# Decays and scaled operands of the recurrent heads made in the projection stage; closing sums of attention on GpSimd and ScalarE

## The chip, the cores and the metric

The kernel runs on one core of a Trainium2 chip as one program. The metric is the device time of one execution in microseconds. Inputs and outputs are float32 in DRAM.

## The reference, cut to what matters

One encoder layer runs over two sequences, 2048 and 256 tokens, of width 1024. A joint projection feeds two mixers side by side: differential attention (4 heads) and a bidirectional RWKV-7 recurrence (8 heads of 64, both directions). The mixed output is projected back, and a squared-ReLU feed-forward of width 4096 follows, each with a residual.

```python
z = rms_norm(x, norm1_g) @ w_in                    # 3328 columns: 1536 attention, 1792 recurrent
# attention: q, k normed and rotated; two softmaxes per head
attn = softmax(q0 k0) - lam * softmax(q1 k1); o = rms_norm(attn @ v, subln_g) * (1 - lambda_init)
# recurrence, d = direction, w_dn/a_dn/g_dn low-rank parts of z after mixing with neighbours
w_log = -softplus(-(w0[d] + tanh(w_dn) @ w_up[d])) - 0.5
decay = exp(-exp(w_log))
a_rate = sigmoid(a0[d] + a_dn @ a_up[d])
kk = normalised(k * k_k);  k_dir = k * (1 + (a_rate - 1) * k_a)
state = state * decay + (state @ -kk) outer (kk * a_rate) + v outer k_dir;  y = state @ r
x = x + concat(o, gate(normed(y) + bonus)) @ w_out
x = x + relu(rms_norm(x, norm2_g) @ w_ff1) ** 2 @ w_ff2
```

## The kernel before, in words

18 tiles of 128 tokens (16 of the long sequence, 2 of the short) go through four stages. Matrix products of the big weights are split into a high and a low part and done in three passes. A scheduler at build time lays out the order of each engine's queue: it takes instructions in program order where it can and moves others up when their inputs and buffers are free by its own estimate of times. Every transfer is issued by SyncE, whose queue is in order as well.

**Projection.** `project_stream` takes two groups of nine tiles. `tall` makes recurrent columns transposed, 128 columns by 384 tokens at a time; `wide` makes attention columns, two tiles by 256 columns per PSUM bank, three banks in turn (tag `mm`). For q and k the result goes to `rope` (L308 on): a Square on ScalarE (L324), a sum on VectorE (L326), a power on GpSimd (L90), the normed tile `qn` (L330, the last reader of the bank), products with cosine and sine (`t1` L333, `t2` L336), their sum (L340), a split into two parts, transposes, a store. `sq` and `t2` share the tag `rsq`. The column blocks of attention go in the order 512, 1024, 768, 1280, 0, 256; blocks under 1024 have a rope for every two tiles, five per block; the last two run as a pair with ten ropes in a row. Weights of a step are loaded in four pieces through `w_raw`, one step ahead.

Between the yields of this stream, `rw_prep` runs for nine blocks of two tiles. It mixes each recurrent column with its neighbours in time (`mix`: one ScalarE and two VectorE operations), makes the low-rank rates for four groups of 128 columns (loop over `c`), and stores plain operands to DRAM: r (RR), kk (KK), k and b of both directions (KB), tanh of the decay's low rank (TW), v (V).

**Attention beside the recurrence.** `merge` in program order interleaves 72 attention items (head, tile) with 18 recurrent units. An item's scores go through VectorE (maximum), ScalarE (exponential), GpSimd and VectorE (difference of the two softmaxes), TensorE (transpose and product with v), and `attn_out` closes it (L640 on). A recurrent unit treats a tile in each direction: `rw_inter` (L873 on) loads the stored operands, makes the decay (a matmul `lp`, tanh, a scan in chunks of 64, two exponentials), multiplies r, kk, k and b by it into `ar` and `bk`, and makes masked scores (`scp`, L935) and transposes; `rw_leaf` inverts 32x32 triangles, `rw_merge` joins them, `rw_chain` runs the state. Preparation is two units ahead of the chain.

**Output projection** (`wout`) and **feed-forward** (`mlp`) follow.

## Time and profile before

| what | us |
|---|---|
| median of 3 runs (4057.95 to 4066.89) | 4065.56 |
| profiled execution, its own time | 4069.43 |
| its span, first to last instruction | 4067.6 |
| TensorE busy / VectorE busy | 3841.0 / 2535.4 |
| ScalarE busy / GpSimd busy | 1904.9 / 1249.5 |
| mean granted clock of TensorE | 0.969 |

Busy time of TensorE is modelled and overlaps from one matmul to the next, so a busy TensorE need not be at its peak. The granted clock is a share of 2.4 GHz. "Idle before" of a group is the time in which its engine stood still just ahead of it, and the arrow names what ended that.

### The profile page before, as it was taken

What the parts mean: (1) busy time and instruction counts of PE and PEld (TensorE: products, weight loads), DVE (VectorE), ACT (ScalarE), POOL (GpSimd) and SP (SyncE); (2) the same over time, 40 slices, a digit from 0 to 9 for tenths busy, and PEclk for the clock granted to TensorE, in tenths of its full rate; (3) what the DMA queues carried; (4) which work ended last, traced back from release to release, by engine and by line L of the source; (5) the groups of instructions that cost most, each with busy time, mean ns of one, the idle gap of its engine ahead of it and who ended that gap; (6) DMA issues with size and microseconds to landing.
All of it is one profiled execution on the core that took longest, in us unless ns stands there. A gap on an engine that the chain in (4) does not pass through costs nothing.

```text
span 4067.6 us, 75970 instructions
## 1 busy us (share of the span) xinstructions
PE 3841.0 (94%) x28790; PEld 3428.7 (84%) x28790; DVE 2535.4 (62%) x5080; ACT 1904.9 (47%) x4312; POOL 1249.5 (31%) x1632
## 2 busy tenths in 40 slices
PE   8999998988889888889897999999999999999999
PEld 8999998976777677777776778999999999999998
DVE  4254767679878878788885775444444444444443
ACT  4354555467666656566665224333333333333332
POOL 0023666556656556556554440000000000000000
PEclk9999998999989989889998999999999999999999
DMA  6366666643443343334324376222252222521221
GB/s 188 121 198 194 199 178 195 181 108 73 111 95 83 94 119 90 85 85 112 89 62 151 105 234 200 63 68 67 63 186 63 64 66 65 158 63 63 63 63 39
DMA packets 617558, 458.05 MB, mean 113 GB/s; under 512 B 232498, under 2 KB 569191, under 8 KB 617192
## 3 DMA queue, kind: packets, MB, share of 16 engines
q1 hardware_dynamic: 617192, 453.20, 38.9%
q8 instruction: 227, 3.72, 0.4%
q14 instruction: 139, 1.14, 0.1%
HBM read 323.98 MB, written 129.07 MB: 111 GB/s over the span
## 4 chain that ended last, share of the span: by engine, by line
PE 54%; DVE 11%; POOL 6%; DMA 4%; issue 3%; ACT 2%; SPq 1%; POOLq 0%; DVEq 0%; ACTq 0%
PE ups L102 7%; PE ups L100 7%; PE ups L101 7%; PE yps L102 6%; PE yps L101 6%; PE yps L100 6%; DVE nb L591 2%; PE oo L637 2%; PE wops L101 2%; PE wops L100 2%; PE wops L102 2%; POOL lx L964 1%; DMA XD<-lx 1%; POOL ltmp L962 1%; DVE lx L964 1%
## 5 line engine op out<-in xcount | busy, mean ns | idle before, releaser
L504 DVE TENSOR_TENSOR acc<-yps,acc 128x512 f32<-128x512 f32 x576 | 392.0, 688 | 374.8 <-PE yps L102 374.8
L100 PE MATMUL ups<-h2hi,f_hi 128*128 128x384 f32 x1536 | 515.6, 336 | 0.0
L102 PE MATMUL ups<-h2hi,f_lo 128*128 128x384 f32 x1536 | 515.6, 336 | 0.0
L101 PE MATMUL ups<-h2lo,f_hi 128*128 128x384 f32 x1536 | 515.3, 335 | 0.0
L595 ACT ACTIVATE P<-sc,nb 128x512 f32<-128x512 f32 (+1 forms) x528 | 360.2, 685 | 218.4 <-DVE nb L591 203.2
L101 PE MATMUL yps<-f_lo,uh 128*128 128x512 f32 x1152 | 449.8, 391 | 0.0
L100 PE MATMUL yps<-f_hi,uh 128*128 128x512 f32 x1152 | 449.6, 391 | 0.0
L102 PE MATMUL yps<-f_hi,ul 128*128 128x512 f32 x1152 | 442.8, 391 | 0.0
L137 ACT CAST f_hi<-f_raw 128x1024 fp32r<-128x1024 f32 x96 | 96.2, 1048 | 646.7 <-PE yps L102 645.3
L591 DVE TENSOR_REDUCE nb<-sc 128x1 f32<-128x512 f32 (+1 forms) x528 | 345.2, 671 | 56.7 <-PE sc L589 55.6
L637 PE MATMUL oo<-vv,at 128*128 128x128 f32 x2080 | 307.0, 294 | 31.5 <-ACT at L634 20.6
L637 PEld LDWEIGHTS oo<-vv,at 128*128 128x128 f32 x2080 | 272.1, 202 | 60.9 <-ACT at L634 31.6
L588 PE MATMUL sc<-kt,qq 128*128 128x512 f32 (+1 forms) x528 | 253.3, 480 | 49.0 <-ACT P L595 42.1
L492 DVE TENSOR_TENSOR ul<-u,uh 128x384 fp32r<-128x384 f32 x192 | 106.8, 556 | 299.8 <-ACT uh L491 296.3
L101 PEld LDWEIGHTS ups<-h2lo,f_hi 128*128 128x128 f32 x1536 | 288.2, 188 | 5.7
L102 PEld LDWEIGHTS ups<-h2hi,f_lo 128*128 128x128 f32 x1536 | 288.2, 188 | 5.5
L100 PEld LDWEIGHTS ups<-h2hi,f_hi 128*128 128x128 f32 x1536 | 288.3, 188 | 5.5
L102 PEld LDWEIGHTS yps<-f_hi,ul 128*128 128x128 f32 x1152 | 216.1, 188 | 47.4
L143 DVE SCALAR_TENSOR_TENSOR f_lo<-f_raw,g,f_hi 128x256 fp32r<-128x256 f32 x384 | 168.7, 481 | 138.6 <-ACT f_hi L142 138.5
L100 PE MATMUL mm<-w_hi,hT_hi 128*128 128x256 f32 x864 | 250.2, 290 | 4.9 <-DVE qn L330 4.2
L100 PEld LDWEIGHTS yps<-f_hi,uh 128*128 128x128 f32 x1152 | 216.3, 188 | 39.3
L101 PE MATMUL mm<-w_lo,hT_hi 128*128 128x256 f32 x864 | 249.0, 289 | 0.0
(236 smaller groups left out, 9313.0 us busy)
## 6 DMA issues: line engine op xcount, KB each, us to landing
f_raw<-w_ff SPq DMA_DIRECT2D x192, 256.0 KB
f_raw<-w_ff SPq DMA_DIRECT2D x96, 512.0 KB
w_raw<-w_in SPq DMA_DIRECT2D x104, 256.0 KB
qq<-QT SPq DMA_DIRECT2D x288, 64.0 KB
kb<-KB SPq DMA_DIRECT2D x36, 512.0 KB
ZT<-zs SPq DMA_DIRECT2D x84, 192.0 KB
xt<-x SPq DMA_DIRECT2D x27, 512.0 KB
zr<-ZT SPq DMA_DIRECT2D x18, 516.0 KB
```

What stands on the lines that cost most here:

```text
L100: mm(ps, lh, rh, start=start, stop=False)
L101: mm(ps, lh, rl, start=False, stop=False)
L102: mm(ps, ll, rh, start=False, stop=stop)
L137: nc.scalar.copy(hi[:, ks], raw)
L143: nc.vector.scalar_tensor_tensor(out=lo[:, k], in0=raw[:, k - k0], scalar=gk, in1=hi[:, k].bitcast(F32), op0=ALU.mult, op1=ALU.subtract)
L492: nc.vector.tensor_tensor(out=ul[:, ns], in0=u2, in1=uh[:, ns].bitcast(F32), op=ALU.subtract)
L504: nc.vector.tensor_tensor(out=acc[j][:, cs], in0=ps, in1=acc[j][:, cs], op=ALU.add)
L588: nc.tensor.matmul(sc, qq[:, c, 0], kt, start=True, stop=False)
L591: nc.vector.tensor_reduce(out=m, in_=sc, axis=AX.X, op=ALU.max, negate=True)
L595: nc.scalar.activation(out=P, in_=sc, func=AF.Exp, bias=m, accum_out=(a["ls"][:, hf] if a["nh"] > 1 else a["l"])[:, c:c + 1])
L637: nc.tensor.matmul(a["op"], at[:, b], a["kv"][1][hf][:, b], start=k == 0, stop=k == a["n"] - 1)
L964: e.tensor_tensor(out=X[:, 0:i, k0:16], in0=X[:, 0:i, k0:16], in1=tmp[:, 0:i, 0:n], op=ALU.add)
```

## The change

The decay and the products with it move from `rw_inter` into the loop over `c` of `rw_prep`. It makes both directions at once, 256 tokens per column group, and stores the scaled operands in the form in which the score matmuls read them: AR and BK take the place of RR, KK, KB and TW. The products of the decay's low rank use a high and a low part in place of one float32 product. V is stored per column group and tile. To make room, several tags go down to one buffer (`rsq`, `hlT`, `kb`), `w_raw` from three to two, and the r vectors are made per column group. In `rw_inter` the two heads' score products no longer alternate. The indices of a tile's two halves are swapped for the backward direction in `rw_chain`. `attn_out` uses GpSimd for the sums and ScalarE for the scaling.

```diff
-            raw = (rp or sp).tile([128, st, shape[2]], F32, name=tag + "_raw", tag=tag + "_raw", bufs=3)
+            raw = (rp or sp).tile([128, st, shape[2]], F32, name=tag + "_raw", tag=tag + "_raw", bufs=RAWB[tag])
...
-        sq = sp.tile([128, m * n, 64], F32, name="rsq", tag="rsq")
+        sq = sp.tile([128, m * n, 64], F32, name="rsq", tag="rsq", bufs=RSQ)
...
-        t2 = sp.tile([128, m, n, 64], F32, name="t2", tag="rsq")
+        t2 = sp.tile([128, m, n, 64], F32, name="t2", tag="rsq", bufs=RSQ)
...
-            hT = sp.tile([128, n, m, 128], F32R, name="hlT", tag="hlT")
+            hT = sp.tile([128, n, m, 128], F32R, name="hlT", tag="hlT", bufs=1)
...
-        nc.vector.scalar_tensor_tensor(out=rs, in0=l0, scalar=1e-6, in1=l0, op0=ALU.mult, op1=ALU.mult)
-        nc.vector.scalar_tensor_tensor(out=rs, in0=ss, scalar=1.0 / 128, in1=rs, op0=ALU.mult, op1=ALU.add)
+        nc.gpsimd.tensor_scalar(out=rs, in0=l0, scalar1=l0, scalar2=1e-6, op0=ALU.mult, op1=ALU.mult)
+        nc.gpsimd.tensor_scalar(out=rs, in0=ss, scalar1=1.0 / 128, scalar2=rs, op0=ALU.mult, op1=ALU.add)
         nc.gpsimd.tensor_tensor(out=rs, in0=rs, in1=self.halfneg[:, 0:1], op=ALU.pow)
         o = sp.tile([128, 128], F32, name="o", tag="ao", bufs=1)
-        nc.vector.tensor_scalar(out=o, in0=op, scalar1=rs, scalar2=None, op0=ALU.mult)
+        nc.scalar.activation(out=o, in_=op, func=AF.Copy, scale=rs)
...
+            for j in range(n):
+                nc.sync.dma_start(out=self.V[t0 + j * 128:t0 + j * 128 + 128].rearrange("p (h c i) -> p h c i", h=2, c=4)[:, :, c], in_=vt[:, j])
...
+                for nm, x, o, bias in (("w_up", (wh, wl), lw, self.w0h), ("a_up", (ah, al), th, self.a0h)):
+                    aps = pp.tile([128, W], F32, name="aps", tag="w512")
+                    aw = wp[nm][:, d, c * 128:c * 128 + 128]
+                    nc.tensor.matmul(aps, aw, x[0], start=True, stop=False)
+                    nc.tensor.matmul(aps, aw, x[1], start=False, stop=True)
+                    nc.scalar.activation(out=o[:, d], in_=aps, func=AF.Tanh, scale=0.5, bias=bias[:, d * 4 + c:d * 4 + c + 1])
+            nc.gpsimd.tensor_scalar(out=lw, in0=lw, scalar1=CDEC, scalar2=CDEC, op0=ALU.mult, op1=ALU.add)
...
+            for d in range(2):
+                x = lw[:, d]
+                nc.vector.tensor_tensor_scan(out=x[:, ::-1] if d else x, data0=self.chunk[:, 0:W], data1=x[:, ::-1] if d else x,
+                                             initial=0.0, op0=ALU.mult, op1=ALU.add)
+                nc.scalar.activation(out=eg[:, d, 0:nq, 1:65], in_=x.rearrange("p (q t) -> p q t", t=64), func=AF.Exp)
+                nc.scalar.activation(out=en[:, d], in_=x, func=AF.Exp, scale=-1.0)
+                e = 1 if d else 64
+                nc.gpsimd.tensor_copy(self.pcs[:, s0 + b0:s0 + b0 + n, d, c], eg[:, d, 0:nq, e:e + 1].rearrange("p (j x) o -> p j (x o)", x=2))
...
+            ar = sp.tile([128, nq, 2, 2, 64], F32, name="aro", tag="aro", bufs=1)
+            nc.gpsimd.tensor_tensor(out=ar[:, :, :, 1].rearrange("p q d t -> p d q t"), in0=rf.rearrange("p (q t) -> p q t", t=64).unsqueeze(1).to_broadcast([128, 2, nq, 64]),
+                                    in1=eg[:, :, 0:nq, 1:65], op=ALU.mult)
+            for d in range(2):
+                nc.vector.scalar_tensor_tensor(out=ar[:, :, d, 0], in0=kq[:, :, ::-1] if d else kq, scalar=-0.5,
+                                               in1=eg[:, d, 0:nq, 65:1:-1] if d else eg[:, d, 0:nq, 0:64], op0=ALU.mult, op1=ALU.mult)
...
+            nc.sync.dma_start(out=self.AR[:, qs, :, c].rearrange("p q d k -> p (q d) k"), in_=ar.rearrange("p q d o t -> p (q d) (o t)"))
+            bk = sp.tile([128, nq, 2, 2, 64], F32, name="kb", tag="kb", bufs=1)
+            for d in range(2):
+                b = bk[:, :, d, 1]
+                nc.vector.scalar_tensor_tensor(out=b[:, :, ::-1] if d else b, in0=th[:, d].rearrange("p (q t) -> p q t", t=64), scalar=1.0, in1=kq, op0=ALU.add, op1=ALU.mult)
+                e = en[:, d].rearrange("p (q t) -> p q t", t=64)
+                nc.vector.tensor_tensor(out=b, in0=b, in1=e[:, :, ::-1] if d else e, op=ALU.mult)
+            nc.gpsimd.tensor_scalar(out=th, in0=th, scalar1=self.ka2[:, cs], scalar2=self.ka1[:, cs], op0=ALU.mult, op1=ALU.add)
...
+            nc.gpsimd.tensor_tensor(out=kd, in0=th, in1=kf[:, c:c + 1].to_broadcast([128, 2, W]), op=ALU.mult)
+            nc.gpsimd.tensor_tensor(out=bk[:, :, :, 0].rearrange("p q d t -> p d q t"), in0=kd.rearrange("p d (q t) -> p d q t", t=64), in1=en.rearrange("p d (q t) -> p d q t", t=64), op=ALU.mult)
+            dst = self.BK[:, qs, :, c].rearrange("p q d k -> p (q d) k")
+            nc.sync.dma_start(out=dst[64:128], in_=bk[64:128].rearrange("p q d s t -> p (q d) (s t)"))
+            for z in range(2):
+                nc.sync.dma_start(out=dst[0:64, :, 64 - 64 * z:128 - 64 * z], in_=bk[0:64, :, :, z].rearrange("p q d t -> p (q d) t"))
...
-        nc.sync.dma_start(out=tw, in_=self.TW[:, ts])
...
-            nc.sync.dma_start(out=ar[:, :, x, 1], in_=self.RR[:, :, t * 128 + xn * 64:t * 128 + xn * 64 + 64].rearrange("c p t -> p c t"))
...
-        nc.sync.dma_start(out=kb, in_=self.KB[:, :, :, d, ts])
...
-            nc.tensor.matmul(lp[:, c], self.wup[:, d, c * 128:c * 128 + 128], tw, start=True, stop=True)
...
-        nc.vector.tensor_tensor_scan(out=en.rearrange("p a b -> p (a b)"), data0=self.chunk, data1=lw[:, ::-1] if d else lw,
...
+        ar, bk = (sp.tile([128, 2, 4, 2, 64], F32, name=nm, tag=nm, bufs=b) for nm, b in (("ar", R), ("bk", 2)))
+        for o, src in ((ar, self.AR), (bk, self.BK)):
+            nc.sync.dma_start(out=o.rearrange("p x c s t -> p x (c s t)"), in_=src[:, 2 * t:2 * t + 2, d].rearrange("p x c k -> p x (c k)"))
...
-            nc.vector.tensor_tensor(out=bk[b, :, :, s], in0=view(kb[b, :, s]), in1=en4[b], op=ALU.mult)
...
+        nc.gpsimd.tensor_copy(pc[:, d], self.pcs[:, t, d, :, ::-1] if d else self.pcs[:, t, d])
...
-            pss = [pp.tile([128, 4, 128], F32, name="scp", tag=SCPT, bufs=WB) for h in range(2)]
-            for c in range(4):
-                for h in range(2):
-                    hs = slice(h * 64, h * 64 + 64)
-                    nc.tensor.matmul(pss[h][:, c], bk[hs, c, x].rearrange("p s t -> p (s t)"),
+            for h in range(2):
+                hs = slice(h * 64, h * 64 + 64)
+                ps = pp.tile([128, 4, 128], F32, name="scp", tag=SCPT, bufs=WB)
+                for c in range(4):
+                    nc.tensor.matmul(ps[:, c], bk[hs, c, x].rearrange("p s t -> p (s t)"),
                                      ar[hs, c, x].rearrange("p s t -> p (s t)"), start=True, stop=True)
-            for h in range(2):
-                nc.vector.tensor_tensor(out=sc[:, h, 4 * x:4 * x + 4], in0=pss[h], in1=self.mask[:, d * (1 + h):d * (1 + h) + 1].to_broadcast([128, 4, 128]), op=ALU.mult)
+                nc.vector.tensor_tensor(out=sc[:, h, 4 * x:4 * x + 4], in0=ps, in1=self.mask[:, d * (1 + h):d * (1 + h) + 1].to_broadcast([128, 4, 128]), op=ALU.mult)
...
+RSQ = 1
+RAWB = {"w": 2, "f1": 3, "f2": 3}
```

## Rows read from the trace of the kernel before

**Rows 1.** Busy time by stage: stretch, us, each engine (count), clock, DMA share, GB/s
```profile
0.00:840.00 840.00, 797.59 (x5654) 784.06 (x5654) 479.57 (x1019) 401.11 (x908) 341.89 (x376) 0.98 0.60 179
840.00:2210.00 1370.00, 1198.58 (x13891) 995.67 (x13890) 1108.43 (x2502) 886.34 (x2216) 796.86 (x1169) 0.93 0.38 92
2210.00:2470.00 260.00, 251.53 (x1174) 198.09 (x1174) 189.27 (x315) 79.96 (x137) 110.24 (x88) 0.98 0.59 195
2470.00:4067.00 1597.00, 1593.31 (x8076) 1450.87 (x8073) 758.13 (x1247) 537.45 (x1054) 0.55 (x1) 1.00 0.26 82
```

**Rows 2.** Chain that ended last, shares of the whole span by engine
```profile
PE 54%; DVE 11%; POOL 6%; DMA 4%; issue 3%; ACT 2%; SPq 1%; POOLq 0%; DVEq 0%; ACTq 0%
```

**Rows 3.** Groups of instructions, VectorE, attention stage 840 to 2210 us
```profile
L900 DVE TENSOR_TENSOR_SCAN en<-chunk,lw 128x512 f32<-128x512 bf16 x36 | 49.1, 1364 | 31.5 <-POOL lw L898 31.5
L914 DVE SCALAR_TENSOR_TENSOR ar<-kk,eg 128x512 f32<-128x512 f32 x36 | 29.0, 805 | 2.5 <-ACT eg L903 2.1
L925 DVE TENSOR_TENSOR bk<-kb,en 64x512 f32<-64x512 f32 x36 | 26.8, 744 | 0.0
L927 DVE TENSOR_TENSOR bk<-kb,en 64x512 f32<-64x512 f32 x36 | 26.2, 729 | 0.5
L649 DVE TENSOR_SCALAR o<-oo,ors 128x128 f32<-128x128 f32 x72 | 24.6, 342 | 13.5 <-POOL ors L647 11.3 <-DMA MIX<-o 1.9
...
L646 DVE SCALAR_TENSOR_TENSOR ors<-oss,ors 128x1 f32<-128x1 f32 x72 | 19.2, 267 | 18.5 <-ACT osq L643 18.1
...
L645 DVE SCALAR_TENSOR_TENSOR ors<-l 128x1 f32<-128x1 f32 x72 | 17.5, 244 | 0.1
...
L917 DVE TENSOR_TENSOR ar<-ar,eg 128x512 f32<-128x512 f32 x18 | 13.6, 755 | 0.0
```

**Rows 4.** The same view, GpSimd
```profile
L922 POOL TENSOR_TENSOR bk<-kb,en 128x512 f32<-128x512 f32 x36 | 49.0, 1382 | 0.5 <-ACT en L904 0.5
L647 POOL TENSOR_TENSOR ors<-ors,halfneg 128x1 f32<-128x1 f32 x72 | 42.6, 592 | 119.3 <-DVE ors L646 116.3 <-DVE lx L964 1.7 <-DVE g L610 0.8
L917 POOL TENSOR_TENSOR ar<-ar,eg 128x512 f32<-128x512 f32 x18 | 23.2, 1291 | 12.5 <-ACT eg L903 9.3 <-DMA XD<-lx 2.9 <-DVE ltmp L962 0.3
L898 POOL TENSOR_SCALAR lw<-lw 128x512 f32<-128x512 f32 x36 | 22.3, 621 | 30.4 <-ACT lw L896 13.0 <-ACT cf L606 12.4 <-DMA MIX<-o 2.7
```

**Rows 5.** The same view, ScalarE
```profile
L903 ACT ACTIVATE eg<-en 128x512 f32<-128x512 f32 x36 | 22.7, 629 | 29.5 <-DVE en L900 26.0 <-DVE mx L604 2.5 <-DVE ors L646 0.8
```

**Rows 6.** Timeline of TensorE, attention stage: start, us, instruction, count in the run
```profile
1513.87 1.16 PE L894 MATMUL lp<-tw,wup 65*128 65x128 f32 x8
...
1530.74 1.16 PE L935 MATMUL scp<-ar,bk 64*128 64x128 f32 x16
1531.83 1.16 PE L637 MATMUL oo<-vv,at 128*128 128x128 f32 x8
...
1536.11 1.16 PE L935 MATMUL scp<-ar,bk 64*128 64x128 f32 x8
```

**Rows 7.** Busy time by stretch, second half of projection; columns as in rows 1
```profile
420.00:780.00 360.00, 338.62 (x2779) 332.43 (x2778) 261.23 (x535) 186.88 (x419) 217.46 (x225) 0.96 0.63 186
600.00:640.00 40.00, 28.94 (x185) 26.64 (x184) 37.51 (x74) 25.94 (x61) 28.51 (x34) 0.76 0.76 223
780.00:828.00 48.00, 48.00 (x416) 48.00 (x415) 23.89 (x46) 14.85 (x27) 29.78 (x23) 1.00 0.61 173
```

**Rows 8.** Groups of instructions, whole run, preparation blocks
```profile
L809 DVE SCALAR_TENSOR_TENSOR kb<-th,rsb 128x256 f32<-128x256 f32 x72 | 35.8, 509 | 21.1 <-ACT th L805 19.1 <-DMA KB<-kb 1.8
...
L805 ACT ACTIVATE th<-aps,a 128x256 f32<-128x256 f32 x72 | 33.7, 472 | 53.3 <-POOL kb L811 33.0 <-PE aps L803 17.1 <-PE mm L102 2.7
```

**Rows 9.** Timeline of all engines, one rope and the next Square
```profile
777.58 0.60 ACT L324 ACTIVATE rsq<-mm 128x512 f32<-128x512 f32 x1 [1.06 <-PE mm L102]
...
783.99 0.60 ACT L324 ACTIVATE rsq<-mm 128x512 f32<-128x512 f32 x1 [5.55 <-PE mm L102]
784.00 0.69 DVE L340 TENSOR_TENSOR t<-t,t 128x512 f32<-128x512 f32 x1 [1.87 <-POOL t L336]
```

**Rows 10.** One line of the tile w_raw: least/median/most ns, first and last start
```profile
L143 DVE SCALAR_TENSOR_TENSOR w_lo<-w_raw,g,w_hi x208: 468/480/1524, 8.7 to 776.3; 128x256 fp32r<-128x256 f32 x104
```

More of the change, by code (lines that the diff above doesn't have):

```diff
@@ L170, in rope_tables @@
             for p in range(2):
-                g = sp.tile([128, 4, 128], F32, name="cst", tag="rsq")
+                g = sp.tile([128, 4, 128], F32, name="cst", tag="rsq", bufs=RSQ)
                 nc.vector.tensor_tensor(out=g, in0=cs, in1=self.gqk[:, p].unsqueeze(1).to_broadcast([128, 4, 128]), op=ALU.mult)
@@ L183, in project_norms @@
         for t in range(t0, t0 + self.NB // 128):
[L184 removed]
+            xt = sp.tile([128, D], F32, name="xt", tag="xt", bufs=XTB)
             self.nc.sync.dma_start(out=xt, in_=self.I["x"][t * 128:(t + 1) * 128])
@@ L527, in lam_params @@
         lam = cp.tile([128, 2], F32, name="lam2")
-        ab = self.rp.tile([128, 2, 2, 64], F32, name="lab", tag="rf", bufs=1)
+        ab = self.rp.tile([128, 2, 2, 64], F32, name="lab", tag="rsb", bufs=1)
         for i in range(2):
@@ L737, in rw_prep @@
             nc.vector.tensor_tensor(out=al[p:p + 64], in0=wa[64:128], in1=ah[64:128].bitcast(F32), op=ALU.subtract)
-        nc.gpsimd.memset(tw[64:65], 1.0)
-        nc.sync.dma_start(out=self.TW[:, ts], in_=tw)
-        zg = sp.tile([128, W], F32, name="zg", tag="zg", bufs=1)
+        wh, wl = (sp.tile([128, W], F32R, name="w" + s, tag="tw" + s, bufs=1) for s in ("hi", "lo"))
+        for p in (0, 64):
+            nc.scalar.copy(wh[p:p + 64], wa[0:64])
+            nc.vector.tensor_tensor(out=wl[p:p + 64], in0=wa[0:64], in1=wh[0:64].bitcast(F32), op=ALU.subtract)
+        zg = sp.tile([128, W], F32, name="zg", tag="wa", bufs=1)
         mix(zr, 1, 13, zg)
@@ L783, in rw_prep @@
         kk = rsb
-        vt = sp.tile([128, n, 2, 4, 64], F32, name="vt", tag="vt", bufs=1)
         todo = []
@@ L812, in rw_prep @@
-            nc.sync.dma_start(out=self.KB[64:128, c, :, :, ts], in_=kb[64:128])
-            for s in range(2):
-                nc.sync.dma_start(out=self.KB[0:64, c, 1 - s, :, ts], in_=kb[0:64, s])
-            bo = sp.tile([128, W], F32, name="kds", tag="kds")
-            nc.gpsimd.tensor_tensor(out=bo, in0=kb[:, 0, 0], in1=kb[:, 0, 1], op=ALU.add)
-            nc.vector.scalar_tensor_tensor(out=bo, in0=rf[:, c], scalar=self.r_k[:, cs], in1=bo, op0=ALU.mult, op1=ALU.mult)
+                for nm, x, o, bias in (("w_up", (wh, wl), lw, self.w0h), ("a_up", (ah, al), th, self.a0h)):
[4 more added lines that the diff above has]
+                    nc.scalar.activation(out=o[:, d], in_=aps, func=AF.Tanh, scale=0.5, bias=bias[:, d * 4 + c:d * 4 + c + 1])
@@ L818, in rw_prep @@
+            for z in range(2):
+                nc.sync.dma_start(out=dst[0:64, :, 64 - 64 * z:128 - 64 * z], in_=bk[0:64, :, :, z].rearrange("p q d t -> p (q d) t"))
+            bo = sp.tile([128, W], F32, name="kds", tag="ksq")
+            nc.gpsimd.tensor_tensor(out=bo, in0=kd[:, 0], in1=kd[:, 1], op=ALU.add)
+            nc.vector.scalar_tensor_tensor(out=bo, in0=rf, scalar=self.r_k[:, cs], in1=bo, op0=ALU.mult, op1=ALU.mult)
             vf = sp.tile([128, W], F32, name="vf", tag="vf")
@@ L890, in rw_inter @@
-        kb = sp.tile([128, 4, 2, 128], F32, name="kb", tag="kb", bufs=1)
-        nc.sync.dma_start(out=kb, in_=self.KB[:, :, :, d, ts])
-        lp = pp.tile([128, 4, 128], F32, name="lp", tag="w", bufs=WB)
-        for c in range(4):
-            nc.tensor.matmul(lp[:, c], self.wup[:, d, c * 128:c * 128 + 128], tw, start=True, stop=True)
-        lw = sp.tile([128, 512], F32, name="lw", tag="bk", bufs=1)
-        nc.scalar.activation(out=lw, in_=lp.rearrange("p c t -> p (c t)"), func=AF.Tanh, scale=0.5)
@@ L897, in rw_inter @@
-        with self.urgent():
-            getattr(nc, LWE).tensor_scalar(out=lw, in0=lw, scalar1=CDEC, scalar2=CDEC, op0=ALU.mult, op1=ALU.add)
-        en = sp.tile([128, 8, 64], F32, name="en", tag="en", bufs=1)
-        nc.vector.tensor_tensor_scan(out=en.rearrange("p a b -> p (a b)"), data0=self.chunk, data1=lw[:, ::-1] if d else lw,
-                                     initial=0.0, op0=ALU.mult, op1=ALU.add)
-        g4 = en.rearrange("p (c x) t -> p c x t", c=4)
-        nc.scalar.activation(out=eg.rearrange("p (c x) t -> p c x t", c=4)[:, :, :, 1:65], in_=g4[:, ::-1] if d else g4, func=AF.Exp)
@@ L918, in rw_inter @@
-        bk = sp.tile([128, 4, 2, 2, 64], F32, name="bk", tag="bk", bufs=1)
-        for s in range(2):
-            if d == 0:
-                with self.urgent():
-                    getattr(nc, D0E).tensor_tensor(out=bk[:, :, :, s], in0=view(kb[:, :, s]), in1=en4, op=ALU.mult)
-                continue
-            k, b = slice(64 - s * 64, 128 - s * 64), slice(s * 64, s * 64 + 64)
-            nc.vector.tensor_tensor(out=bk[b, :, :, s], in0=view(kb[b, :, s]), in1=en4[b], op=ALU.mult)
-            kx = kb[k, :, s].rearrange("p c (x t) -> p c x t", x=2)
-            nc.vector.tensor_tensor(out=bk[k, :, :, s], in0=kx[:, :, ::-1], in1=en4[k, :, :, ::-1], op=ALU.mult)
+        nc.gpsimd.tensor_copy(pc[:, d], self.pcs[:, t, d, :, ::-1] if d else self.pcs[:, t, d])
```

109 lines of the change are left out of this document (42 added, 67 removed).

## The prediction

> **What bounds the kernel now.** I read the busy table by stage first, then the chain of waits, then groups of instructions. [rows 1] cut the run at the last projection matmul, the end of attention and the end of the output projection: projection 840 us, attention beside the recurrent heads 1370, output projection 260, feed-forward 1597. TensorE is busy for 95% of the first, 97% of the third and all of the last; the change touches neither of the last two. In attention TensorE shows 1199 of 1370 us, VectorE 1108 (81%), ScalarE 886, GpSimd 797, at a granted clock of 0.93 of the 2.4 GHz level. The chain in [rows 2] gives VectorE 11% of the 4067.6 us span (447 us) and GpSimd 6% (244); as the other stages run on TensorE, nearly all of that lies in attention. There no engine is full; VectorE is the one waited for most.
>
> **What goes from attention.** A tile of 128 tokens and a direction is one unit of recurrent preparation: 18 x 2 = 36. VectorE loses per unit the scan, the products into ar and bk, and in 72 closings of a head three small operations. The VectorE rows of [rows 3] add up: 49.1 + 29.0 + 26.8 + 26.2 + 13.6 = 144.7 us for decays and products, 24.6 + 19.2 + 17.5 = 61.3 for closings: 206 of 1108 us, 19%. GpSimd loses 49.0 + 23.2 + 22.3 = 94.5 us [rows 4] and gains 144 one-column operations; none is in the trace, so between 0 and the 592 ns of the power on the same column [rows 4]; I take 0.25 us, 36 us, as these only multiply (with the 36 small copies of pc some 45). ScalarE loses three passes of about 0.63 us per unit [rows 5], 68 us, and gains 72 scalings of a 128x128 tile, at the 342 ns that VectorE takes for it 25 us. A closing hops ScalarE, GpSimd, ScalarE instead of ScalarE, VectorE, GpSimd, VectorE, but now queues behind GpSimd's 1.3 us products and behind exponentials; the next head's output matmuls wait for it. I count that as nothing: between -13.5 us (the wait for ors before o in [rows 3]) and +72 x 1.3 = 94 if each met a product.
>
> TensorE loses the 8 decay instructions of a unit and gets a new order in its score products. In [rows 6] one run of 16 instructions L935, with both heads of a pair alternating, starts at 1530.74 and the next group at 1531.83: 1.09 us. The other half of the unit went as two runs of 8, one head each, of the same 1.16 us each. A run of 8 with one head costs as much as 16 with both. After the change heads are always one after the other, as one PSUM bank is taken at a time: 36 x 1.09 = 39 us more. The decay products lp are 8 instructions, 1.16 us in [rows 6] too: 39 us less. TensorE's work in the stage stays the same, so it does not pay for the stage; its idle time must.
>
> The loads of a unit fall from five (tw, kk, two ar, kb) to two with packets four times as long. I count nothing for that: DMA is at 0.38 there [rows 1].
>
> Gain: if VectorE's 447 us on the chain shrink as its work does, 19% = 85 us; GpSimd net (94.5 - 45) / 797 = 6% of 244 = 15; 100 together. Another path stands next each time (leaf steps, DMA through DRAM, TensorE), so I take four fifths: **-80 us**. Bounds: 0 if TensorE's unchanged work is the limit, -206 if the stage follows VectorE alone.
>
> **What comes into projection.** Nine blocks of preparation, four column groups c each. TensorE: 9 x 4 x 2 x 2 = 144 decay matmuls of 256 columns. In the undisturbed 48 us after 780 there are 416 matmuls, most of that size [rows 7], 0.115 us each: **+17 us**, uncovered, since TensorE is full.
>
> VectorE per c: two scans of 256 (half of 1364 ns), two products for a and two more for b at the 509 ns of L809 [rows 8], plus 18 small splits: 72 x (0.68 + 2 x 0.51) + 9 = 131 us; 480 becomes 611 of 840. GpSimd per c: one scaling of lw (621 ns) and two products of 512 (1382 ns) [rows 4]; the paired th and kd operations become one each of double width, which I let cancel the two tiny copies: 36 x 3.4 = 122 us, 342 becomes 464. ScalarE: six passes of 472 ns [rows 8] per c, two tanh and four exp, 102 us, 401 becomes 503.
>
> Of the nine blocks I put five inside 420 to 780 [rows 7]. There VectorE goes from 261 to 261 + 5/9 x 131 = 334 of 360 us (93%), GpSimd from 217 to 285 (79%). What a full VectorE does is seen already: from 600 to 640 it is busy 37.5 of 40 us, TensorE falls to 28.9 and the clock to 0.76 [rows 7]. Those two rows are why I do not take the engines as cover.
>
> GpSimd and VectorE also stand in each other's way: the split of w takes 468 ns at least, 480 in the median and 1524 at most [rows 10]. The Trainium skill, page SBUF — State Buffer, section SBUF: two separate sides, calls their common port pair an exclusive lock that the first comer holds for a whole instruction, so that a GpSimd operation blocks a VectorE operation with two SBUF inputs. By that rule the 122 us more of GpSimd could cost VectorE up to 122 us. The trace agrees that one is held up, 1524 against 480 ns, but shows it seldom. If VectorE's 131 us stretch by a tenth (an estimate: the median of the 208 splits lies 12 ns over the least, so most meet nothing), that is 13 us, half of it hidden; I charge **8** for VectorE's stretch and backlog on TensorE, between 0 and 40.
>
> The buffers pay too. rsq falls from two to one, and Square's result and t2 of the rope share it. So the Square of the next pair of tiles, which begins the release of its PSUM bank, must wait until the add L340 of this pair has read t2. In the quietest stretch [rows 9] a Square starts at 777.58, its L340 ends at 784.69: 7.1 us. The next Square starts at 783.99, 6.4 us later, as TensorE delivers. The loop is longer than the supply, so 40 ropes in runs of five and ten become serial. Behind the waiting Square stand ScalarE's queue (copies of PSUM, tanh, exp) and after three banks TensorE. With work of other kinds between the steps I take 8.7 us for the loop against 6.2 of supply; two further banks cover 12 us. Runs of five (5 x 2.5 = 12) are covered; two runs of ten lack 25 - 12 = 13 each: 26, with 4 for the lower clock after a stall (0.76 in [rows 7]) **+30**. Bounds: 2 at the quiet loop of 7.1, and at a loop of 10.5, with the loaded engines above, 2 x (43 - 12) + 3 x (21.5 - 12) = 90.
>
> Other buffers (w_raw three to two, hlT two to one) add waits of a DMA where weights are made a step ahead; nothing, up to 10 us at the ends of paired steps. Stores grow: the operands of both directions of ar are now written, and V goes in 72 short stores instead of 9, in an SP queue that also carries the weight loads; DMA stands at 0.60 [rows 1], and I count nothing, up to +15.
>
> Sum: projection 17 + 8 + 30 = +55; attention -80; net -25. The profiled execution took 4069.43 us (span 4067.6): 4044. The median of the runs, 4065.56, lies 3.9 lower, so **4040 us**.
>
> **Rivals.** (A) Slower: the rope loop on one buffer decides. For it: 7.1 us already in quiet [rows 9], and queues fuller by a quarter. At 10.5 us it costs 90; with 17 and 20 of backlog projection gains 127, attention gives back 70: +57, 4122. Against it: TensorE's stalls let the other engines catch up. It turns the sign from a loop of about 9.4 us, where the two runs of ten lack 40 and the runs of five 4 each, 52 together, and projection reaches 77.
> (B) Attention gains more: VectorE's queue was the reason for most idle time, and shorter waits also bring the clock up from 0.93. Attention -135, projection +40: 3970.
> (C) The change of place gives nothing: TensorE's 39 us for the separated heads fall on the chain, its lost 39 did not lie there, GpSimd's closings hold up the output matmuls. Attention -40, projection +45: 4070.
>
> **How the numbers follow.** 0.2% (8 us) is about what a measurement here can tell from no change. My case 0.50 (4000 to 4075; of this 0.43 faster, 0.05 same, 0.02 slower); B 0.17, all faster; C 0.13 (0.05 same, 0.08 slower); A 0.20, slower. Together faster 0.60, same 0.10, slower 0.30. The range 3968 to 4108 takes in C, most of B, and the near half of A.
>
> **What would show it.** Right: the last projection matmul near 880 us instead of 828; Squares in a run of ten 8 to 9 us apart and each starting right after an L340; VectorE in attention near 900 us in a stage of about 1290; L935 only in runs of 8, near 1.1 us each. Wrong: Squares 6.4 us apart (the buffer did not bind), or over 10 (A); an attention stage above 1340 (C) or below 1245 (B).

## The result, and the profile after

The changed kernel takes 4158.6 us (median of 4 runs, 4150.5 to 4164.0), beside 4066.2 us for the kernel before on the same chip: a ratio of 1.0228 (95% interval 1.0204 to 1.0253). It is 2.3% slower, where 4040 us was predicted, and it lies above the range. The profiled execution took 4155.4 us, with a span of 4153.7.

Busy time by stage, with the cuts at the last projection matmul, the end of attention and the end of the output projection, as in [rows 1]:
```profile
0.00:1034.00 1034.00, 876.84 (x5782) 849.84 (x5783) 683.84 (x1247) 484.39 (x1139) 469.97 (x473) 0.92 0.54 154
1034.00:2277.00 1243.00, 1158.91 (x13614) 955.80 (x13613) 917.31 (x2130) 849.53 (x2146) 711.97 (x1260) 0.97 0.40 100
2277.00:2542.00 265.00, 250.40 (x1184) 199.75 (x1185) 188.68 (x317) 77.81 (x139) 112.79 (x89) 0.97 0.59 197
2542.00:4154.00 1612.00, 1607.26 (x8070) 1462.51 (x8068) 757.39 (x1246) 536.94 (x1053) 0.56 (x1) 1.00 0.26 81
```
Nearly all of the loss stands in the first row. By the exact places of the cuts the projection went from 828.2 to 1034.2 us (+206), attention from 1372.7 to 1242.3 (-130), the output projection from 269 to 265 and the feed-forward stage from 1592.8 to 1607.6 (+15): together +86, the difference of the two spans. TensorE has nearly the same work in the projection and is busy for 85% of it instead of 95%, at a granted clock of 0.92 of the 2.4 GHz level instead of 0.98. VectorE is busy 684 us there instead of 480.

The chain that ended last, by engine, answers to [rows 2]:
```profile
PE 59%; DVE 6%; DMA 4%; POOL 3%; issue 1%; ACT 1%; SPq 1%; POOLq 0%; DVEq 0%; ACTq 0%
```
VectorE fell from 11 to 6%, GpSimd from 6 to 3%. In attention the change did more than was claimed for it. VectorE's longest wait of that stage, before and after (in total, times, longest):
```profile
DVE nb L591 <- PE sc L589: 55.6, 59, 4.7
```
```profile
DVE nb L591 <- PE sc L589: 144.9, 123, 5.0
```

VectorE's groups in the projection (line, engine, operation, out and in, count, busy us, mean ns, idle before) answer to [rows 8, 10]:
```profile
L143 DVE SCALAR_TENSOR_TENSOR w_lo<-w_raw,g,w_hi 128x256 fp32r<-128x256 f32 x208 | 126.1, 642 | 97.6 <-ACT w_hi L142 96.1 <-DMA ZT<-zs 1.2
L811 DVE TENSOR_TENSOR_SCAN lw<-chunk,lw 128x256 f32<-128x256 bf16 x72 | 60.1, 874 | 3.9 <-POOL lw L807 3.8
L834 DVE TENSOR_TENSOR kb<-kb,lw 128x256 f32<-128x256 f32 x72 | 49.5, 710 | 0.6 <-ACT lw L814 0.2
L832 DVE SCALAR_TENSOR_TENSOR kb<-th,rsb 128x256 f32<-128x256 f32 x72 | 38.9, 566 | 15.6 <-DMA BK<-kb 13.2 <-issue 2.1 <-ACT th L806 0.2
...
L825 DVE SCALAR_TENSOR_TENSOR aro<-rsb,eg 128x256 f32<-128x256 f32 x72 | 31.0, 454 | 2.8 <-DMA AR<-aro 1.8 <-ACT lw L814 0.8
```
L811, L834 and L825 are new. The split of the weights, L143, is not: the same 208 instructions took 526 ns in the mean before (median 480 in [rows 10]) and take 642 now. Before:
```profile
L143 DVE SCALAR_TENSOR_TENSOR w_lo<-w_raw,g,w_hi 128x256 fp32r<-128x256 f32 x208 | 100.5, 526 | 95.8 <-ACT w_hi L142 95.7
```
Two of these pieces beside two products on GpSimd in the changed kernel (start, us):
```profile
302.40 2.94 DVE L143 SCALAR_TENSOR_TENSOR w_lo<-w_raw,g,w_hi 128x256 fp32r<-128x256 f32 x2
302.29 1.34 POOL L837 TENSOR_TENSOR th<-th,kf 128x512 f32<-128x512 f32 x1
303.71 1.36 POOL L838 TENSOR_TENSOR kb<-th,lw 128x512 f32<-128x512 f32 x1
```
Each of the two lasts about as long as the product beside it.

What TensorE waits for from 430 to 1034 us (in total, times, longest):
```profile
PE rtps L350 <- DVE hl L343: 38.1, 14, 7.3
PE mm L100 <- DVE qn L330: 22.5, 15, 5.6
PE cps L786 <- DVE kds L845: 20.8, 10, 8.4
```
Before, none of these exceeded 4.2 us. All three end at VectorE: its rope and its preparation come late. One rope after the other, answering to [rows 9]:
```profile
660.00 0.69 DVE L340 TENSOR_TENSOR t<-t,t 128x512 f32<-128x512 f32 x1 [1.88 <-POOL t L336]
...
677.91 1.78 DVE L340 TENSOR_TENSOR t<-t,t 128x512 f32<-128x512 f32 x1
```
```profile
651.45 0.59 ACT L324 ACTIVATE rsq<-mm 128x512 f32<-128x512 f32 x1
661.68 0.59 ACT L324 ACTIVATE rsq<-mm 128x512 f32<-128x512 f32 x1
680.26 0.59 ACT L324 ACTIVATE rsq<-mm 128x512 f32<-128x512 f32 x1
```
Each Square starts 0.6 to 1.0 us after the L340 before it ends (660.69, 679.69), and the next ones come 10.2 and 18.6 us apart. Over the whole run, 36 of the 39 later Squares start within 2.3 us behind the L340 before them; the other three open a block.

### The profile page after: what moved, and what is told of

Its sections match the earlier page's. It is cut to its first block, busy times and chain, and to the rows that moved or that the text cites. A ratio compares the mean times of both kernels' runs of the same rounds, so it can differ in the third digit from the quotient of the medians.

```text
span 4153.7 us, 75665 instructions
## 1 busy us (share of the span) xinstructions
PE 3893.4 (94%) x28646; PEld 3467.9 (83%) x28646; DVE 2547.2 (61%) x4938; ACT 1948.7 (47%) x4475; POOL 1295.3 (31%) x1822
## 4 chain that ended last, share of the span: by engine, by line
PE 59%; DVE 6%; DMA 4%; POOL 3%; issue 1%; ACT 1%; SPq 1%; POOLq 0%; DVEq 0%; ACTq 0%
PE ups L100 7%; PE ups L101 7%; PE ups L102 7%; PE yps L102 6%; PE yps L101 6%; PE yps L100 6%; PE oo L637 3%; PE scp L921 3%; PE sc L588 2%; PE atp L632 2%; PE wops L101 2%; PE wops L102 2%; PE wops L100 2%; PE sc L589 1%; DVE nb L591 1%
## 5 line engine op out<-in xcount | busy, mean ns | idle before, releaser
L591 DVE TENSOR_REDUCE nb<-sc 128x1 f32<-128x512 f32 (+1 forms) x528 | 347.0, 676 | 154.5 <-PE sc L589 152.5
L100 PE MATMUL mm<-w_hi,hT_hi 128*128 128x256 f32 x864 | 263.6, 306 | 22.7 <-DVE qn L330 22.5
L101 PE MATMUL mm<-w_lo,hT_hi 128*128 128x256 f32 x864 | 261.4, 303 | 2.1 <-DVE w_lo L143 2.1
L102 PE MATMUL mm<-w_hi,hT_lo 128*128 128x256 f32 x864 | 260.9, 302 | 0.0
L588 PE MATMUL sc<-kt,qq 128*128 128x512 f32 (+1 forms) x528 | 243.3, 461 | 17.7 <-ACT P L595 12.9
L143 DVE SCALAR_TENSOR_TENSOR f_lo<-f_raw,g,f_hi 128x256 fp32r<-128x256 f32 x384 | 168.7, 482 | 142.5 <-ACT f_hi L142 142.5
```

The source lines that it names most:

```text
L100: mm(ps, lh, rh, start=start, stop=False)
L101: mm(ps, lh, rl, start=False, stop=False)
L102: mm(ps, ll, rh, start=False, stop=stop)
L143: nc.vector.scalar_tensor_tensor(out=lo[:, k], in0=raw[:, k - k0], scalar=gk, in1=hi[:, k].bitcast(F32), op0=ALU.mult, op1=ALU.subtract)
L588: nc.tensor.matmul(sc, qq[:, c, 0], kt, start=True, stop=False)
L591: nc.vector.tensor_reduce(out=m, in_=sc, axis=AX.X, op=ALU.max, negate=True)
```

## The experiments

Times are medians; the kernel before was run beside each group of runs (4057.5 to 4061.3 us), and ratios with their 95% intervals are to it. The changed kernel itself was run only beside the 4066.2 us of the first group. A difference from its 4158.6 us is therefore uncertain by some 9 us, and the traces' spans are given beside it. e6, e12, e14 and e16 leave out work of the layer; they only show what it costs. "Projection" is the start of the last projection matmul in the trace.

### One rope buffer, and the other buffers

**e1**: the changed kernel with two rsq buffers.
```
-RSQ = 1
+RSQ = 2
```


> The changed kernel with two buffers for rsq again, all else as changed. Theory 1 (the rope's loop on one buffer sets the projection stage): Squares no longer wait for the previous L340, the last projection matmul comes near 900 us instead of 1034, the total falls by about 110 to 130 us to 4030 to 4050. Theory 2 (VectorE and GpSimd are full with the work that came in, the buffer only shows it): the stage stays above 990 us and the total above 4115.

4122.5 us, 1.0160 (1.0133 to 1.0188): 36 us back by the medians, 28 by the ratios, 34 by the traces. Projection 977 instead of 1034; attention gave 23 of these 57 us up again (1242 to 1266). The result lies between the two theories: the buffer is part of the loss, not the whole.

**e2**: the kernel before with one rsq buffer (`bufs=1` on everything with that tag).

> The kernel before with one buffer for rsq and nothing else changed. Theory 1: Squares in a run stand one loop apart (9 to 10 us instead of 5 to 6.5), the last projection matmul moves from 828 to 880 or later, the total rises by 50 to 70 us to 4115 to 4135. Theory 2: without the added work the engines catch up and the total rises by less than 15 us.

4148.8 us, 1.0226 (1.0202 to 1.0251): 91 us by this cut alone (74 by the traces: 53 in the projection, 22 in attention). That is theory 1, and more than it expected in total. In the projection the cut costs the old kernel about what it costs the new one, 53 against 57. The totals differ in attention, which is 22 us longer here and 23 shorter from e1 to the changed kernel; why is not shown.

**e7**: the kernel before with the two other cuts, and the feed-forward stage's buffers moved.
```
-hT = sp.tile(... tag="hlT")
+hT = sp.tile(... tag="hlT", bufs=1)
-raw = (rp or sp).tile(... bufs=3)
+raw = (rp or sp).tile(... bufs=2 if tag == "w" else 3)
+pad = self.ma.tile([128, 296], F32, name="pad")
```


> The kernel before with the change's two other cuts of buffers alone: hlT at one buffer, the raw weights of the projection at two. If these buffers are part of the loss: the projection goes from 828 to 840 or more (and a slower kernel by 12 us or more); as the prediction has it: nothing up to 10 us. Besides, a spare tile of 1184 B ahead of the MLP's buffers puts them at exactly the addresses that they have in the changed kernel. If the place makes the 15 us: the MLP goes from 1592.8 to 1607 us here, with nothing else of the change in it; otherwise it stays at 1592.8.

4102.3 us, 1.0095 (1.0076 to 1.0113). Projection 845, 17 us more; attention 6 more; the feed-forward stage exactly 1607.6, with nothing else of the change in it. So these buffers are part of the loss.

### VectorE and GpSimd in the preparation

All of these have two rsq buffers; compare them with e1's 977.

**e5**: two scalings from GpSimd to ScalarE, and the feed-forward's buffers moved back.
```
-nc.gpsimd.tensor_scalar(out=lw, in0=lw, scalar1=CDEC, scalar2=CDEC, ...)
+nc.scalar.activation(out=lw, in_=lw, func=AF.Identity, scale=self.cdec[:, 0:1], bias=self.cdec[:, 0:1])
-nc.gpsimd.tensor_scalar(out=th, in0=th, scalar1=self.ka2[:, cs], ...)
+nc.scalar.activation(out=th, in_=th, func=AF.Identity, scale=self.ka2[:, cs], bias=self.ka1[:, cs])
+pad = self.ma.tile([128, 720], F32, name="pad")
```


> The changed kernel with two rsq buffers (4122.5 us when run before), and the two scalings of the preparation (L807 and L835: 36 x 702 ns and 36 x 1303 ns, 72 us of GpSimd) given to ScalarE, which is 475 of 977 us busy in the projection. Theory P (GpSimd, by running beside VectorE, stretches VectorE's operations; it decides): VectorE's mean durations fall, its busy time in the projection from 655 towards 635 us and the projection from 977 to about 955. Theory L (VectorE's own added instructions decide): VectorE keeps 650 us and the projection stays within 8 us of 977. Besides, a spare tile of 2880 B ahead of the MLP's buffers puts them back at the same place modulo 4096 bytes as in the kernel before; if their place against the weights' buffers at the other end of the memory makes the MLP's 15 us, the MLP goes from 1607.6 to 1593 us; if it is anything else, it stays at 1607.6.

4087.9 us, 1.0066 (1.0051 to 1.0081). Projection 976 and VectorE 656: as theory L has it. The gain is the feed-forward stage (1592.8) and 24 us in attention, which I did not expect.

**e6**: the scans left out.
```
-nc.vector.tensor_tensor_scan(out=x[:, ::-1] if d else x, ...)
```


> The changed kernel with two rsq buffers, and the running sums of the decays (L811, 72 scans of 874 ns, about 60 us of VectorE, some 600 us of the projection's span in which they lie) left out: the exponentials run on the decays themselves, so this part of the computation is missing. Nothing is taken from GpSimd or TensorE. Theory L (VectorE's added instructions decide): the projection goes from 977 to 920 to 935 us, two thirds or more of the 60. Theory Q (what decides is that each step of preparation comes as one block in the engines' order, with GpSimd's chain of four products behind each other): under 25 us.

4081.7 us, 1.0055 (1.0040 to 1.0070). Projection 938, 3 us outside what theory L expected: 40 us for 40 us of VectorE's busy time.

**e12**: the scans, L825 and L834 left out; the a operand is one fixed tile of zeros.

> The changed kernel with two rsq buffers, and all that the change added to VectorE in the projection apart from the split of the decay's operand left out: the scans (72 x 901 ns in the run of e1), the products of the b operand with the inverse decay (72 x 658) and those of the a operand with the decay (72 x 498); 144 us by e1's trace. So the decays are not summed, and a is zero: this part of the computation is missing. TensorE's, ScalarE's and GpSimd's work and all DMAs stay. Theory L, at e6's rate (one us of projection for one of VectorE): the projection goes from 977 to 835 to 865 us, which is the kernel before (828) with what its other two buffers cost (17 in e7) and the 17 us of the decay's own products: nothing else is then left to explain. Theory Q (GpSimd's chain and blocks of preparation): the projection stays above 900 us.

4055.3 us, 0.9991 (0.9981 to 1.0000). Projection 908, which is theory Q's side (above 900), far from theory L's 835 to 865; yet 70 us went, three fifths of the 113 us that VectorE's busy time lost.

**e14**: e12 with GpSimd's added work left out too; the k and b operand is then a fixed tile as well.
```
-nc.gpsimd.tensor_scalar(out=lw, ...)
-nc.gpsimd.tensor_copy(self.pcs[...], eg[...])
-nc.gpsimd.tensor_tensor(out=ar[:, :, :, 1] ...)
-nc.gpsimd.tensor_tensor(out=bk[:, :, :, 0] ...)
```


> The kernel of e12 (projection 907.7 us), and GpSimd's added work in the preparation left out too: the decay's scaling (36 x 0.7 us), the copies of the chunk ends (72 x 0.4), the product of the r operand (36 x 1.37) and the products of the k operand with the inverse decay (36 x 1.37); some 150 us of GpSimd. What the change still adds to the projection is then TensorE's decay products, ScalarE's tanh and exponentials, the split of the decay's operand, the stores, and the smaller buffers. Theory P' (GpSimd's work in the preparation's chain holds what is left of the loss): the projection falls from 908 to 860 to 880 us. Theory B (buffers, TensorE's own products and ScalarE hold it): it stays above 895. Besides, a spare tile of 32 B ahead of the MLP's buffers: if the 64-byte step decides, the MLP is 1592.8 us instead of 1607.6.

4066.1 us, 1.0010 (0.9999 to 1.0022), projection 953: no answer. With nothing left to wait for, 35 operand stores went out at the start. From 60 to 150 us (TensorE busy in the first column, DMA share next to last but one):
```profile
60.00:150.00 90.00, 25.08 (x124) 23.55 (x122) 9.09 (x18) 9.30 (x18) 2.25 (x5) 0.64 1.02 274
```
TensorE is busy 25 of 90 us there; in e12 it is busy for all 90.

**e16**: e14 with each store tied to its step by a small copy.
```
+nc.gpsimd.tensor_copy(ar[:, :, :, 1, 0:1]..., eg[:, :, 0:nq, 1:2])
+nc.gpsimd.tensor_copy(bk[:, :, :, 0, 0:1]..., kd...[:, :, :, 0:1])
```


> The kernel of e14 with the one fault of e14 mended: there the stores of the a and r operands hung on nothing in the preparation, 35 of them went out at the start, and TensorE lost some 70 us between 60 and 150 us. Now two small copies (4 columns of each chunk row, on GpSimd) stand in the place of the two products left out, so that each store waits for its own step. Theory P' (GpSimd's added work in the preparation holds what is left of the loss): a projection of 860 to 885 us instead of e12's 908. Theory B (buffers, TensorE's decay products, ScalarE hold it): 895 or more.

3986.5 us, 0.9824 (0.9808 to 0.9839). Projection 874, as theory P' has it. The projection of e1, e6, e12 and e16, columns as in [rows 1]:
```profile
0.00:977.30 977.30, 859.42 (x5745) 836.51 (x5746) 654.42 (x1211) 475.81 (x1108) 467.75 (x459) 0.93 0.55 156
```
```profile
0.00:937.60 937.60, 838.60 (x5738) 819.91 (x5738) 615.04 (x1145) 473.07 (x1110) 449.80 (x462) 0.95 0.57 163
```
```profile
0.00:907.70 907.70, 828.88 (x5733) 812.34 (x5734) 541.22 (x999) 468.89 (x1101) 426.52 (x457) 0.96 0.59 167
```
```profile
0.00:873.90 873.90, 812.10 (x5762) 798.33 (x5762) 498.60 (x1015) 480.28 (x1115) 322.79 (x366) 0.98 0.64 181
```
From the third to the fourth no VectorE instruction was removed (1015 fall in the stretch, against 999), yet VectorE's busy time fell from 541 to 499 us as GpSimd's fell from 427 to 323. L143 in e12 and in e16:
```profile
L143 DVE SCALAR_TENSOR_TENSOR w_lo<-w_raw,g,w_hi 128x256 fp32r<-128x256 f32 x208 | 115.4, 594 | 107.5 <-ACT w_hi L142 107.1
```
```profile
L143 DVE SCALAR_TENSOR_TENSOR w_lo<-w_raw,g,w_hi 128x256 fp32r<-128x256 f32 x208 | 98.2, 508 | 112.0 <-ACT w_hi L142 111.7
```

### Order, pace and a nearer version

**e3**: the changed kernel with the heads' score products alternating, as before (two PSUM tiles, the loop over heads inside that over c).

> The changed kernel with the two heads' score products alternating again as before (two PSUM banks taken at once). If TensorE's time in attention is on the path: runs of 16 return, 39 us of TensorE go, and the attention stage shortens by 15 to 39 us. If it is not: within 8 us. The projection stage stays at 1034.

4136.4 us, 1.0196 (1.0172 to 1.0221): 22 us back by the medians, 13 by the ratios, 23 by the traces, 17 of these in attention. The edit brought back only a part of the old order. TensorE's busy time on the score products (first number behind the length) in the kernel before, the changed one and e3:
```profile
828.00:2201.00 1373.00, 139.10 (x1152) 116.91 (x1152) 95.98 (x144) 0.93 0.38 91
1034.00:2277.00 1243.00, 166.82 (x1152) 136.71 (x1152) 97.91 (x144) 0.97 0.40 100
1029.00:2255.00 1226.00, 156.38 (x1152) 126.96 (x1152) 96.96 (x144) 0.97 0.40 101
```
The separated heads added 28 us, and e3 took back 10 of them, not the 39 that it expected.

**e8**: e1's kernel with the column step cut in two.
```
+yield
-PREP_RATE = 1.35
+PREP_RATE = 1.8
```


> The changed kernel with two rsq buffers, and each column step of the preparation cut in two (a yield ahead of the key products, the rate raised from 1.35 to 1.8 steps for each of the projection's so that it ends as early). The work is the same. Theory Q (blocks of preparation queued ahead of the rope loop on VectorE): the median Square-to-product loop falls from 15.5 to about 11 us and the projection from 977 to 940 to 960. Theory L (load): within 10 us of 977.

4134.9 us, 1.0183 (1.0168 to 1.0198). Projection 957, but the preparation ended at 1015 us instead of 1001, and attention's first product came at 1038. The 20 us lie in what theory Q expected, but the median loop only fell from 15.5 to 13.5 us, and the whole got slower than e1: no answer on the block form, and nothing gained by it.

**e9**: e5 with e3's order.

> The kernel of e5 (two rsq buffers, the two scalings on ScalarE, the MLP's buffers put back; 4087.9 us) with the score products of the recurrent heads in the order of the kernel before, the two heads alternating, so that neighbouring products use different row halves. If the order costs what e3 showed on the changed kernel (22 us), independently of the rest: 4066 us, within 6 us of the kernel before. If VectorE has become what paces attention there, less than 10 us: 4078 or more.

4076.4 us, 1.0047 (1.0033 to 1.0061): 11 us below e5 by the medians, 8 by the ratios, between the two expectations. In attention the two edits do add up: the stage is 16 us shorter than e5's (1242 to 1225), as it was 17 shorter in e3.

**e10**: e9 with `PREP_RATE = 1.55`.

> The kernel of e9 with the preparation issued faster, 1.55 steps for each step of the projection instead of 1.35, so that it ends before the projection does: in e5 the last preparation ended at 970 us, the last projection product at 976 and the first attention product at 989; in the kernel before they were 781, 828 and 828. If the gap of 13 us at the seam is a cost of its own: 8 to 13 us below e9. If VectorE's load decides wherever it lies: within 4 us of e9, with a longer projection and no gap.

4067.7 us, 1.0023 (1.0009 to 1.0037). The gain is there, not for the reason given: the last projection matmul came 31 us earlier (946), but the preparation still ended at 975 and the first attention product came at 995. The seam:
```profile
945.00:990.00 45.00, 8.91 (x52) 7.69 (x51) 27.02 (x43) 12.61 (x27) 24.84 (x34) 0.56 0.67 173
```
TensorE is busy for 9 of these 45 us. In the kernel before, the preparation ended at 781 and the matmuls at 828. Its nine blocks ended 63 us apart there; in the changed kernel it is 85.

**e11**: e9 with one scan of 512 columns for both directions (the backward one stored reversed).
```
+l2 = lw.rearrange("p d t -> p (d t)")
+nc.vector.tensor_tensor_scan(out=l2, data0=self.chunk[:, 0:2 * W], data1=l2, ...)
```


> The kernel of e9 with the decays of both directions summed by one scan of 512 columns instead of two of 256 (the backward one is stored reversed; one product on GpSimd becomes two halves). The scan of 512 columns in the kernel before took 1.225 us, the two of 256 columns 2 x 0.87 to 0.93 us: some 0.55 us x 36 = 20 us less VectorE in the projection. By theory L, and at the rate of e6 (40 us of VectorE, 40 us of projection): 15 to 20 us below e9, and the output stays the reference's. By theory Q: under 8 us.

4081.9 us, 1.0064 (1.0042 to 1.0086). Projection 24 us shorter (953), attention 39 longer: 6 us above e9 where 15 to 20 below were expected, a miss.

**e17**: e11 with `PREP_RATE = 1.55`.

> The kernel of e10 (ratio 1.0023 to the kernel before) with the one scan of e11 in place of two: 20 us less VectorE in the preparation. If VectorE's time in the projection is paid one for one and the preparation ends as much earlier: 10 to 20 us below e10, 4048 to 4058 us, level with the kernel before or just under it. If attention takes it back, as from e9 to e11: 4065 or more.

4062.1 us, 1.0008 (0.9999 to 1.0018): level with the kernel before, 2.2% below the changed one by the ratios, and the fastest complete version of it. It is not faster than the kernel before. It is 6 us below e10, between the two expectations.

### Closings

**e4**: the kernel before with the closing sums on GpSimd and ScalarE, as in the change.

> The kernel before with the closing sums of attention on GpSimd and ScalarE, nothing else. If VectorE's load paces the attention stage: 61 of 1108 us of VectorE go and the stage shortens by 20 to 40 us, total 4025 to 4045. If the closings get stuck behind GpSimd's products and hold up the next output matmuls: 0 to 40 us slower.

4063.2 us, 1.0017 (1.0006 to 1.0027): VectorE lost 44 us of busy time in attention, and the stage kept its length (1371 against 1373). So either VectorE's load does not pace that stage in the kernel before, or the new closings take back what the load gives; the run does not tell which.

**e15**: e10 with them back on VectorE.

> The kernel of e10 (two rsq buffers, scalings on ScalarE, heads alternating, faster rate, MLP's buffers put back; 1.0023 of the kernel before) with the closing sums of attention back on VectorE, as in the kernel before. If they cost nothing, as the prediction has it: within 4 us of e10. If e4 carries over (closings on GpSimd and ScalarE cost 6 us there): 4 to 8 us below e10, level with the kernel before. If VectorE paces attention here too: above e10 by some 10 us or more (44 us more of VectorE).

4086.5 us, 1.0065 (1.0042 to 1.0088): 19 us above e10 (17 by the ratios), 23 of them in attention by the traces: the third of the expectations. With the change, the closings on the other engines are worth something.

### The place of the feed-forward's buffers

**e13**: the kernel before with 32 spare bytes ahead of them.

> The kernel before with nothing changed but a spare tile of 32 B ahead of the MLP's buffers. e7 showed that moving them by 1184 B makes the MLP's 15 us. 1184 is 18.5 x 64. If the half of a 64-byte step in which the buffers begin is what matters: the MLP goes from 1592.8 to 1607.6 us and the kernel is 15 us (0.36%) slower. If it is their distance from other buffers in larger units: it stays at 1592.8.

4060.8 us, 0.9997 (0.9986 to 1.0008); the stage 1594.0, so the half of a 64-byte step is not it.

**e18**: e10 with them at 2048 bytes beyond the old place instead of 4096.

> The kernel of e10 with the MLP's buffers 2048 B beyond their place in the kernel before, instead of 4096 B. So far the MLP took 1592.8 us at 0 and 4096, 1594.0 at 32, 1605.4 at 1216 and 1607.6 at 1184. If the place counts modulo 2048 bytes: 1592.8 us and the time of e10. If modulo 4096 or more: another value, between 1575 and 1610 us, with the rest as in e10.

4069.3 us, 1.0023 (1.0013 to 1.0034); the stage 1592.8, as at 0 and 4096.

## Why the prediction was wrong

**Attention, -80: right in kind, too small.** It gave 130 us by the cuts; the first attention product already starts at 1009 us, so 25 of these lie beside the end of the projection and 105 are the stage's own. VectorE's work there was predicted near 900 us and is 917. The step that failed here is that its 447 us on the chain would shrink as its work does, by 19%: 6% of the span is 249 us, 44% less. The granted clock also rose from 0.93 to 0.97. What is late next is TensorE: VectorE waits 145 us for its scores, 56 before. This is what rival B described, at -135; no run separates its two parts. The change also gives the loaded `bk` a second buffer in this stage, which the sum does not price and no run tests. That the separated heads cost TensorE time was right in sign; they added 28 us where [rows 6] gave 39. The closings counted as nothing were level on the kernel before (e4) and worth 19 us with the change (e15).

**Projection, +55: the step that failed; it cost 206.** By removing one thing after the other, in this order (another order could share the time out differently):
```
                                  predicted   measured (run)
one rsq buffer                          30          57  (e1)
VectorE's three added operations    \               70  (e12)
GpSimd's added operations           /   8           34  (e16)
decay products on TensorE               17  \
other buffers, stores, ScalarE           0  /       46  left in e16 (874 against 828)
```
The 8 us "for VectorE's stretch and backlog on TensorE, between 0 and 40" is the term that broke: 70 and 34 us in its place. I had put VectorE at 93% of the stretch from 420 to 780 and priced only the queueing around it. VectorE's busy time rose by 204 us, not 131: the three kinds that I priced at 49, 37 and 37 took 60, 50 and 31, the small splits 14 instead of 9, and some 50 us came from instructions that were there before, such as L143 (526 to 642 ns). I read [rows 10] by its median and least, and missed that its mean, 526 ns in the kernel before, already lay well above both; the sum over 208 pieces follows the mean. The delay of the preparation, whose every block became 22 us longer, was no term of the sum at all: in e1 attention's first product came 41 us after the last projection matmul (1018 against 977), in the kernel before at once.

The stretch is GpSimd's doing. In e16, without its added work, L143 took 508 ns. The traces show it piece by piece as well. Of L143's 208 pieces in the changed kernel, 47 met a GpSimd operation on two tensors (a product or sum, the short powers not counted) and took 1161 ns in the mean; 148 met neither that nor a scaling and took 481. In the kernel before 30 met one and took 798; 151 met neither and took 479. Counted in this way over VectorE's instructions in the projection, each kind against its own median with neither beside it, the stretch was 35 us before, 138 in the changed kernel, 97 in e12 and 54 in e16. So about half of VectorE's 204 us more is stretch, where the prediction had 13. Its own added work was priced too high: alone, the scans took 668 ns instead of 680, the products 418 instead of 509.

The page SBUF — State Buffer of the Trainium skill, section SBUF: two separate sides, has GpSimd and VectorE share a port pair that the first comer holds for a whole instruction; by it the prediction allowed up to 122 us and took 13. The traces agree with it for operations on two tensors, where the 103 us more of stretch come near that bound, and so does e16, with 43 us less of VectorE's busy time for 104 less of GpSimd's. They do not show that scalings with one tensor operand hold VectorE up: the pieces that met only such a scaling lost 8 us in all in the changed kernel. In e5, 58 us less of GpSimd, all of it such scalings, left VectorE's time as it was.

**The rope loop, +30:** the mechanism was right, and each Square does wait for an L340; the size was not. In the changed kernel the loop was not 8.7 us; Squares came 10 to 19 us apart at 650 to 680 us, past the point from which rival A decides. In e2, with no other change, the loop was 8.3 us in the median, near the 8.7 assumed, and the projection still lost 53: by the Squares' places some 38 in the two runs of ten, where 26 was expected, and 11 in the runs of five, where nothing was. (There are four runs of five, not the three in the bound of 90.) The sign and the place are rival A's, its 4122 us still 37 short, as it gave the preparation's load 20 us and the two below nothing. **Other buffers**, nothing up to 10: 17 in the projection on the kernel before (e7). **The feed-forward stage**, which the change was said not to touch, cost 15: the change made the tiles that live through the whole run 1184 bytes larger (`pcs` 1152, `w0h` 32) and so moved its buffers. Its first matmuls took 339 ns instead of 336, here and in e7, which has the same move and neither the new work nor the single rsq buffer.

**Open:** of the 46 us, 17 may be e7's and some 17 the decay products by price; those and the rest were not tried apart on the changed kernel, nor were the single `kb` buffer and the tiles that now share a tag. That e11's attention is longer than e9's with the same work is not explained; the written order of TensorE's instructions differs between the two from within the projection on.

## What to carry to other kernels

Price work moved to a stage by that stage's fullest engine: here 0.6 to 1 us of span for each us of VectorE (e12, e6), and a quarter of what VectorE gained in busy time came from instructions that had not changed. Take the mean of a contended instruction, not its median, and look at what a smaller buffer does before anything else. Better still, split its durations by what the other engine ran beside it: the trace before already held 30 pieces of L143 at 798 ns and the rest near 480. A chain that runs beside the main work, as the preparation here, has a slack (47 us) that is a term of the sum.

## What the runs showed of the hardware

The time of the feed-forward stage depends on where its operands lie in the on-chip memory, although no engine's work changed. With its buffers moved by 0, 32, 1184, 1216, 2048 and 4096 bytes against the first matrix's weights, which stayed, it took 1592.8, 1594.0, 1607.6, 1605.4, 1592.8 and 1592.8 us, the same to 0.1 us wherever a move was run twice. So the runs fit a pattern that repeats at 2048 bytes or a part of it; what makes it is not known. The products of the first matrix start 173 ns apart in the median at 0 and 177 at 1184, those of the second 227 and 228. The first kind of its matmuls in e5 (moved by 4096) and in e7 (by 1184):
```profile
L100 PE MATMUL ups<-h2hi,f_hi 128*128 128x384 f32 x1536 | 515.7, 336 | 0.0
```
```profile
L100 PE MATMUL ups<-h2hi,f_hi 128*128 128x384 f32 x1536 | 520.4, 339 | 0.0
```

GpSimd's operations on two tensors hold up VectorE's instructions with two inputs in the on-chip memory, in the changed kernel's projection by 138 us in all. An instruction that reads PSUM alone is not held up: in the kernel before, up to 1040 us, L591 took 680 ns in the mean in 40 pieces beside such an operation, and 679 in the median in 51 pieces beside none. GpSimd's scalings hold VectorE up hardly at all (8 us there), but they become longer themselves: in the kernel before, the scaling of `th` on GpSimd took 552 ns in the median in 11 pieces with VectorE busy for less than 15% of them, and 954 in the other 61.
